# Mixer A on one Trainium2 core: scores from stacked rounded keys, queries split on POOL, and the division of the last pairs behind the values

## The chip, the core and the metric

The kernel runs on one core of one Trainium2 chip. Its engines are TensorE (PE; the profile lists its weight loads as PEld), VectorE (DVE), ScalarE (ACT), GpSimd (POOL) and SyncE (SP), whose queue issues all of the kernel's DMAs. Each engine takes its instructions in the order in which they were written for it and waits for the others by semaphores. The metric is the device time of one execution in microseconds; less is better.

## What is computed

One inference step of a one-layer streaming encoder on 1024 prompt tokens and 32 sample tokens, 1024 wide, all in fp32: a feed-forward network (FFN), two attention mixers side by side, a second FFN. Each of the three has its normalizations and its scale, shift and gate from a condition. Mixer A, cut to what matters:

```python
# mixer A: 8 heads of 64; a frame reads its own chunk of 64 and the 8 before it
def band_attn_a(qa, ka, va, bias, valid):
    s = einsum('bnqhd,bnkhd->bnhqk', qa, ka) * SCALE + bias
    s = where(valid, s, -1e30)
    p = softmax(s, axis=-1)
    return einsum('bnhqk,bnkhd->bnqhd', p, va)
# mixer B: 8 query heads on 2 key heads, own chunk and 2 before, with a sink in the softmax
o = concat(rmsnorm(oa, gains_a), rmsnorm(ob, gains_b)) @ w_out
```

The newest rows of the keys and values of both mixers are outputs too.

## The kernel before

Tokens lie in three blocks (384, 384 and 288 with the sample), features on partitions. A projection multiplies split operands: `split_w` and its like round a weight to fp32r on ACT (hi) and take the remainder on DVE (lo), and `mm3` sums hi x hi, hi x lo and lo x hi in three matmuls of fp32r. The FFNs, the input and the output projections are made that way (lines 325 to 327, and 669 to 671 for the values). Weights, keys, queries and values live in `wpool`, eight buffers of 8 KB per partition.

Between the FFNs stands the attention: a list of 72 tiles, each of 128 queries and one pair of heads. First come mixer B's four pairs, a sample tile (`TileS`) and eight of `TileB` each, then mixer A's pairs 0 and 1, a sample tile and eight of `TileA` each, then pairs 2 and 3 side by side. Tile `i` of mixer A reads up to 640 keys: its score length L is 128, 256, 384 and 512 for `i` from 0 to 3, and 640 from there on.

A tile of mixer A goes through these steps. `pre` makes a zero-padded copy `qz` of the queries for each head on POOL (lines 741, 742). `qk` multiplies it with the pair's keys in fp32 (line 752, in pieces of up to 512 columns), adds the bias and takes the maximum on DVE, takes the exponential on ACT with its sum (line 761), and divides P by that sum in one pass over it, on ACT or DVE (lines 764, 766). `tr` transposes P on PE (776) and copies PT out of PSUM, `av` multiplies PT with the values (713) into the one PSUM bank `po`, which ACT or DVE copies to O. In mixer B, `split_q` rounds the queries already, with SPLIT = "vav": a rounded copy on DVE, one on ACT and the remainder on DVE, into `qs`; its keys KSB are stacked, rounded keys on 64 partitions and their remainder on the other 64, so that two matmuls make the three products (813, 814).

```python
for e, o in ((SPLIT[0], T[hp, h, :]), (SPLIT[1], T[op, h, :])):
    ...
(ge if SPLIT[2] == "g" else ve).tensor_tensor(lo, q[hp], T[hp, h, :], op=OP.subtract)
```

Between the tiles stand other works, a little at each half tile: from tile 0 to 34 the projections of mixer B's other queries, of the values and of pair 0, from tile 37 to 54 those of pairs 1 to 3 (`pq`). Group norms begin at tile 55 (`sq`, `pss`, `pr`, `z`), and pieces of the output projection (`wo`) stand between the very last tiles. So pairs 2 and 3 have hardly any projections beside them. `k_rows` transposes the newest keys for the output (995). `qs`, PT, `sq`, `z`, the normalized `n` and the rows of keys share five buffers (`hpool`), `qz` has its own five (`spool`), scores have two pairs of PSUM banks.

The order of each engine isn't written out. The program names the steps in an order, and a planner that simulates the engines with its own costs then sets the sequence of each of them; only SP's queue is kept as written, up to the first FFN. So whatever changes a cost or a buffer can change the order on all engines.

## Time and profile before

| | us |
|---|---|
| median of 3 runs (lowest to highest) | 2216.33 (2215.64 to 2218.37) |
| the profiled execution | 2217.6 |
| its span, first to last instruction | 2215.8 |
| PE busy in it | 2161.6 (98%) |
| DVE, ACT, POOL busy | 1239.1, 697.8, 179.2 |

The profiled execution is 1.3 us above the median, and 1.8 us of it lie outside its span. To read the profile: a matmul is pipelined, so the duration of one is longer than its share of PE's time; what one of a row of equal matmuls costs is the distance of their starts. An fp32 matmul has two records in the trace, an fp32r matmul one. An idle time is put down to what ended last before it. The granted clock of PE is 1 at 2.4 GHz and 0.5 at 1.2 GHz.

### The profile page before, as it was taken

The page shows a single profiled execution, that of the slowest core. Times are in us where ns is not written, and L with a number is a line of the kernel's source. Part 1 is how long each engine was busy: PE and PEld are TensorE (multiplying, and loading weights), DVE is VectorE, ACT ScalarE, POOL GpSimd, SP SyncE. Part 2 cuts the span into 40 slices and gives each one's busy share as a digit, 9 for nine tenths or more (in the row PEclk, how much of TensorE's full clock was granted, in tenths as well). Part 3 has the DMA queues.
Part 4 walks back from the last instruction along what each step waited for, and adds up shares of the span by engine and source line. Part 5 has one row for each costly group of instructions (what it writes and reads, how often), then busy time and mean ns, then how long its engine had stood idle before and what let it go on. Part 6 is the DMA issues. An engine that isn't in the chain of part 4 may idle for free.

```text
span 2215.8 us, 33976 instructions
## 1 busy us (share of the span) xinstructions
PE 2161.6 (98%) x14012; PEld 2068.6 (93%) x14012; DVE 1239.1 (56%) x2425; ACT 697.8 (31%) x1450; POOL 179.2 (8%) x281
## 2 busy tenths in 40 slices
PE   6999999999999999899999899999999999999998
PEld 4999999999999999799787589999999999999998
DVE  5788667874333497677444865785333333333336
ACT  4411111111121253576444663542111111111133
POOL 1100000000000023001110313220000000000000
PEclk8999999999999999899999899999999999999999
DMA  9253334434122352111112121424211111111122
GB/s 323 93 153 118 111 96 124 143 101 129 39 66 69 101 184 93 38 39 30 50 30 62 46 77 67 134 86 120 66 58 39 57 39 39 58 38 58 39 69 79
DMA packets 200623, 186.03 MB, mean 84 GB/s; under 512 B 7597, under 2 KB 169813, under 8 KB 199317
## 3 DMA queue, kind: packets, MB, share of 16 engines
q1 hardware_dynamic: 200468, 183.87, 27.1%
q8 instruction: 110, 1.80, 0.3%
q14 instruction: 45, 0.36, 0.1%
HBM read 164.12 MB, written 22.86 MB: 84 GB/s over the span
## 4 chain that ended last, share of the span: by engine, by line
PE 90%; DVE 4%; DMA 3%; ACT 1%; issue 1%; POOL 0%; SPq 0%; ACTq 0%; DVEq 0%; POOLq 0%
PE dn L325 7%; PE dn L326 7%; PE dn L327 7%; PE gate L327 7%; PE gate L326 7%; PE up L327 7%; PE up L326 7%; PE gate L325 7%; PE up L325 7%; PE po L713 3%; PE S L752 2%; PE pq L325 2%; PE pq L327 2%; PE pq L326 2%; DMA raw<-in_w_gate_dram 1%; PE pp L776 1%
## 5 line engine op out<-in xcount | busy, mean ns | idle before, releaser
L326 PE MATMUL gate<-h_lo,w 128*128 128x384 f32 (+1 forms) x1056 | 340.2, 322 | 4.0 <-DVE h_lo L446 4.0
L325 PE MATMUL dn<-gg,w 128*128 128x384 f32 (+1 forms) x1056 | 341.4, 325 | 1.1 <-DVE facc L581 1.0
L581 DVE TENSOR_TENSOR facc<-dn,facc 128x768 f32<-128x768 f32 (+1 forms) x240 | 212.9, 889 | 230.2 <-PE dn L327 229.9
L326 PE MATMUL dn<-gg,w 128*128 128x384 f32 (+1 forms) x1056 | 340.6, 323 | 0.6 <-DVE gg L554 0.6
L325 PE MATMUL gate<-h_hi,w 128*128 128x384 f32 (+1 forms) x1056 | 341.0, 323 | 0.0
L327 PE MATMUL gate<-h_hi,w 128*128 128x384 f32 (+1 forms) x1056 | 340.4, 322 | 0.0
L325 PE MATMUL up<-h_hi,w 128*128 128x384 f32 (+1 forms) x1056 | 340.2, 322 | 0.0
L326 PE MATMUL up<-h_lo,w 128*128 128x384 f32 (+1 forms) x1056 | 340.0, 322 | 0.0
L327 PE MATMUL dn<-gg,w 128*128 128x384 f32 (+1 forms) x1056 | 340.0, 322 | 0.0
L327 PE MATMUL up<-h_hi,w 128*128 128x384 f32 (+1 forms) x1056 | 339.9, 322 | 0.0
L304 DVE TENSOR_TENSOR w<-raw,w 128x1024 fp32r<-128x1024 f32 x187 | 231.5, 1246 | 150.5 <-ACT w L303 150.3
L303 ACT ACTIVATE w<-raw 128x1024 fp32r<-128x1024 f32 x187 | 195.7, 1056 | 266.1 <-PE dn L327 103.5
L550 ACT ACTIVATE sl<-gate 128x384 f32<-128x384 f32 (+1 forms) x132 | 60.9, 462 | 563.9 <-PE gate L327 560.9
L551 DVE TENSOR_TENSOR sl<-sl,up 128x384 f32<-128x384 f32 (+1 forms) x132 | 68.5, 519 | 292.1 <-PE up L327 286.1
L326 PEld LDWEIGHTS gate<-h_lo,w 128*128 128x128 f32 x1056 | 198.6, 188 | 4.6 <-DVE h_lo L446 4.6
L325 PEld LDWEIGHTS dn<-gg,w 128*128 128x128 f32 x1056 | 199.2, 189 | 1.6 <-DVE facc L581 1.2
L326 PEld LDWEIGHTS dn<-gg,w 128*128 128x128 f32 x1056 | 199.2, 189 | 1.0 <-DVE gg L554 0.9
L327 PEld LDWEIGHTS dn<-gg,w 128*128 128x128 f32 x1056 | 199.1, 189 | 0.0
L325 PEld LDWEIGHTS gate<-h_hi,w 128*128 128x128 f32 x1056 | 198.7, 188 | 0.1
L327 PEld LDWEIGHTS gate<-h_hi,w 128*128 128x128 f32 x1056 | 198.7, 188 | 0.0
L327 PEld LDWEIGHTS up<-h_hi,w 128*128 128x128 f32 x1056 | 198.7, 188 | 0.0
L325 PEld LDWEIGHTS up<-h_hi,w 128*128 128x128 f32 x1056 | 198.5, 188 | 0.0
(224 smaller groups left out, 3367.4 us busy)
## 6 DMA issues: line engine op xcount, KB each, us to landing
raw<-in_w_mod_dram SPq DMA_DIRECT2D x56, 512.0 KB, 4.0
raw<-in_w_gate_dram SPq DMA_DIRECT2D x54, 512.0 KB, 4.0
raw<-in_w_up_dram SPq DMA_DIRECT2D x54, 512.0 KB, 4.7
raw<-in_w_down_dram SPq DMA_DIRECT2D x54, 512.0 KB, 4.5
raw<-in_w_in_dram SPq DMA_DIRECT2D x18, 512.0 KB, 4.3
wm<-in_w_mod_dram SPq DMA_DIRECT2D x8, 1024.0 KB, 7.4
raw<-in_w_out_dram SPq DMA_DIRECT2D x13, 512.0 KB, 4.5
xr<-xs SPq DMA_DIRECT2D x16, 384.0 KB, 3.5
```

The costliest lines, as they stand in the source:

```text
L303: ae.activation(w[:, 0], r, AF.Copy)
L304: ve.tensor_sub(w[:, 1], r, w[:, 0])
L325: te.matmul(ps, w[:, 0, k], hi, start=start, stop=False)
L326: te.matmul(ps, w[:, 0, k], lo, start=False, stop=False)
L327: te.matmul(ps, w[:, 1, k], hi, start=False, stop=stop)
L550: ae.activation(sl[:, :w], ps[0][:, :w], AF.Silu)
L551: ve.tensor_tensor(sl[:, :w], sl[:, :w], ps[1][:, :w], op=OP.mult)
L581: ve.tensor_tensor(o, ps[:, :, :w], o, op=OP.add)
L713: te.matmul(po[64 * h:64 * h + 64, :n], vsl(j, h, kn), PT(h, j, kn), start=j == 0, stop=j == nt - 1)
L752: te.matmul(S[:, c:ce], self.T[:, h, :], KQ[:, 0, 128 * k0 + c:128 * k0 + ce], start=True, stop=True)
L776: te.transpose(pp[:, j - j0, :], P[:, 128 * j:128 * j + 128], ident)
```

## The change

The scores of mixer A are made as those of mixer B already were. For each head of a pair the key projection leaves a stacked tile `KS`: ACT rounds the head's keys onto its own 64 partitions, DVE writes the remainder onto the other 64. `pre` fills `qs` with `split_q`: rounded queries on both halves, their remainder on one, zeros on the other. `qk` then takes two fp32r matmuls for each piece of keys; a length of 640 is cut in two pieces of 320, each in a bank of its own, and the shorter lengths are one piece. `k_rows` gets the keys back with a matmul against `twice`, two identities on top of each other, which adds the two halves.

SPLIT becomes "ggg": both rounded copies and the remainder of a query come from POOL, in mixer A and in mixer B. From RNORM = 2 on (pairs 2 and 3) P isn't divided. The reciprocals of a tile's two sums go through two small fp32 matmuls, which lay them along the queries in the same bank `po`; ACT copies them to O, and DVE multiplies the values' product by them.

`wpool` has sixteen buffers of 4 KB in place of eight of 8 KB, and everything in it is cut to that size: a weight's hi and lo are two tiles, a pair's keys two and its queries one, w_mod's first chunks come in four DMAs of half the size.

```diff
+RNORM = 2
...
-SPLIT = "vav"
+SPLIT = "ggg"
...
-    wpool = ctx.enter_context(tc.tile_pool(name="wpool", bufs=8))
+    wpool = ctx.enter_context(tc.tile_pool(name="wpool", bufs=16))
...
+    twice = consts.tile([128, 64], F32R, name="twice")
+    for h in range(2):
+        ae.activation(twice[64 * h:64 * h + 64], ident[64 * h:64 * h + 64, 64 * h:64 * h + 64], AF.Copy)
...
-        w = wpool.tile([128, 2, 8, 128], F32R, name="w", tag="w")
-        ae.activation(w[:, 0], r, AF.Copy)
-        ve.tensor_sub(w[:, 1], r, w[:, 0])
+        w = [wpool.tile([128, 8, 128], F32R, name="w", tag="w") for _ in range(2)]
+        ae.activation(w[0], r, AF.Copy)
+        ve.tensor_sub(w[1], r, w[0])
...
+                if put and not st:
+                    put(ps[:, a:b], slice(t0 + a, t0 + b))
+                    continue
...
-    def av(PT, L, vsl, O_dst, n=128):
+    def av(PT, L, vsl, O_dst, n=128, rden=None):
         po = pc("po")
+        if rden is not None:
+            for h in range(2):
+                te.matmul(po[64 * h:64 * h + 64, 128:256], rden[:, h:h + 1].to_broadcast([128, 64]), ident,
+                          start=True, stop=True)
         nt = (L + 127) // 128
         for j in range(nt):
             kn = min(128, L - 128 * j)
             for h in range(2):
                 te.matmul(po[64 * h:64 * h + 64, :n], vsl(j, h, kn), PT(h, j, kn), start=j == 0, stop=j == nt - 1)
-        evac(O_dst, po[:, :n])
+        if rden is None:
+            evac(O_dst, po[:, :n])
+        else:
+            ae.activation(O_dst, po[:, 128:256], AF.Copy)
+            ve.tensor_tensor(O_dst, po[:, :n], O_dst, op=OP.mult)
...
-            T = self.T = s_tile([128, 2, 128], "qz")
-            cols = slice(128 * self.i, 128 * self.i + 128)
+            q = kqa[self.p]["q"][:, 128 * self.i:128 * self.i + 128]
+            T = self.T = h_tile([128, 4, 128], "qs", F32R)
             for h in range(2):
-                hp, op_ = slice(64 * h, 64 * h + 64), slice(64 - 64 * h, 128 - 64 * h)
-                ge.memset(T[op_, h, :], 0.0)
-                ge.tensor_copy(T[hp, h, :], kqa[self.p][0][hp, 1, cols])
+                ge.memset(T[64 - 64 * h:128 - 64 * h, 2 + h, :].bitcast(F32), 0.0)
+                split_q(T, h, q, T[64 * h:64 * h + 64, 2 + h, :])

         def qk(self, h):
             p, i, k0, L = self.p, self.i, self.k0, self.L
-            KQ = kqa[p][0]
+            K = kqa[p]["k"][h]
             bias = prep[("A", p)]["bias"]
             bw = min(L, 256)
-            S = p2("S", (128, 1024))
-            for c in range(0, L, 512):
-                ce = min(L, c + 512)
-                te.matmul(S[:, c:ce], self.T[:, h, :],
-                          KQ[:, 0, 128 * k0 + c:128 * k0 + ce], start=True, stop=True)
-            ve.tensor_tensor(S[:, L - bw:L], S[:, L - bw:L], bias[:, h, 256 - bw:256], op=OP.add)
+            m = (L + 511) // 512
+            S = p2("S")[:, :m, :L // m]
+            for c in range(m):
+                keys = K[:, 128 * k0 + c * L // m:128 * k0 + (c + 1) * L // m]
+                te.matmul(S[:, c], self.T[:, h, :], keys, start=True, stop=False)
+                te.matmul(S[:, c], self.T[:, 2 + h, :], keys, start=False, stop=True)
+            near = S[:, m - 1, L // m - bw:L // m]
+            ve.tensor_tensor(near, near, bias[:, h, 256 - bw:256], op=OP.add)
             if i >= 4:
-                ve.memset(S[64:128, 0:64], NEG)
+                ve.memset(S[64:128, 0, 0:64], NEG)
             nm = small.tile([128, 1], F32, name="nm")
-            ve.tensor_reduce(nm, S[:, :L], axis=AX.X, op=OP.max, negate=True)
-            den = small.tile([128, 1], F32, name="den")
+            ve.tensor_reduce(nm, S, axis=AX.XY, op=OP.max, negate=True)
+            if p >= RNORM:
+                if h == 0:
+                    self.rden = small.tile([128, 2], F32, name="rden")
+                den = self.rden[:, h:h + 1]
+            else:
+                den = small.tile([128, 1], F32, name="den")
             P = g_tile([128, 640], "P")
-            ae.activation(P[:, :L], S[:, :L], AF.Exp, bias=nm, accum_out=den)
+            ae.activation(P[:, :L].rearrange("p (c n) -> p c n", c=m), S, AF.Exp, bias=nm, accum_out=den)
             ve.reciprocal(den, den)
-            if (2 * i + h) % SC[1] < SC[0]:
+            if p >= RNORM:
+                pass
+            elif (2 * i + h) % SC[1] < SC[0]:
                 ae.activation(P[:, :L], P[:, :L], AF.Copy, scale=den)
             else:
                 ve.tensor_scalar(P[:, :L], P[:, :L], den, None, op0=OP.mult)
...
-               lambda j, h, kn: vt[:, k0 + j, vo + 64 * h:vo + 64 * h + 64],
-               O[tb][:, p, 128 * c:128 * c + 128])
+               lambda j, h, kn: vt[(k0 + j) // 4][:, (k0 + j) % 4, vo + 64 * h:vo + 64 * h + 64],
+               O[tb][:, p, 128 * c:128 * c + 128], rden=self.rden)
...
-        if p % 2 == 0:
-            qb["t"] = wpool.tile([128, 2, 1024], F32, name="qbt", tag="w")
-        qt = qb["t"][:, p % 2, :]
+        qt = wpool.tile([128, 1024], F32, name="qbt", tag="w")
...
-        KQ = wpool.tile([128, 2, 1024], F32, name="KQ", tag="w")
+        KS = [wpool.tile([128, 1024], F32R, name="KS", tag="w") for _ in range(2)]
         KQs = small.tile([128, 2, DEC], F32, name="KQs", bufs=3)
-        kqa[p] = (KQ, KQs)
-        piece = qk_proj(w, KQ[:, 0, :], KQs[:, 0, :], 1.0)
+        kqa[p] = {"k": KS, "s": KQs}
+
+        def put(ps, cols):
+
+            for h in range(2):
+                hp, op = slice(64 * h, 64 * h + 64), slice(64 - 64 * h, 128 - 64 * h)
+                ae.activation(KS[h][hp, cols], ps[hp], AF.Copy)
+                ve.tensor_tensor(KS[h][op, cols], ps[hp], KS[h][hp, cols], op=OP.subtract)
+
+        piece = qk_proj(w, None, KQs[:, 0, :], 1.0, put)
         for tb in range(3):
             yield from piece(tb)

     def flow_qa(p, w):
-        KQ, KQs = kqa[p]
-        piece = qk_proj(w, KQ[:, 1, :], KQs[:, 1, :], 0.125)
+        Q = kqa[p]["q"] = wpool.tile([128, 1024], F32, name="Q", tag="w")
+        piece = qk_proj(w, Q, kqa[p]["s"][:, 1, :], 0.125)
         for tb in range(3):
             yield from piece(tb)

     def k_rows(p):
-        KQ, KQs = kqa[p]
+        KS, KQs = kqa[p]["k"], kqa[p]["s"]
         kr = h_tile([128, 4, 128], "kr")
         pk = (p1 if PB[0] else pc)("pkr", (128, 4, 128))
         for j in range(4):
-            te.transpose(pk[:, j, :], KQ[:, 0, 512 + 128 * j:640 + 128 * j], ident)
+            for h in range(2):
+                te.matmul(pk[:, j, 64 * h:64 * h + 64], KS[h][:, 512 + 128 * j:640 + 128 * j], twice,
+                          start=True, stop=True)
...
-        if p % 2 == 0:
-            prep["aux"] = wpool.tile([128, 2, 2, 4, 128], F32, name="aux", tag="w")
-        aux = prep["aux"][:, p % 2]
+        aux = wpool.tile([128, 2, 4, 128], F32, name="aux", tag="w")
```

PE's order in pairs 2 and 3, some tiles of 640 columns, before (S are the scores, pp the transposes, po the values, pr a group norm):

```order
L752 MATMUL S<-KQ,qz 128x512
L752 MATMUL S<-KQ,qz 128x128
L776 MATMUL pp<-ident,P 128x128 x5
L713 MATMUL po<-PT,vt 64x128 x8
L752 MATMUL S<-KQ,qz 128x512
L752 MATMUL S<-KQ,qz 128x128
L776 MATMUL pp<-ident,P 128x128
L713 MATMUL po<-PT,vt 64x128
```

The same place after, where rden are the reciprocals:

```order
L766 MATMUL S<-KS,qs 128x320
L767 MATMUL S<-KS,qs 128x320
L766 MATMUL S<-KS,qs 128x320
L767 MATMUL S<-KS,qs 128x320
L798 MATMUL pp<-ident,P 128x128 x5
L718 MATMUL po<-ident,rden 64x128 x2
L724 MATMUL po<-PT,vt 64x128
L766 MATMUL S<-KS,qs 128x320
L767 MATMUL S<-KS,qs 128x320
L766 MATMUL S<-KS,qs 128x320
L767 MATMUL S<-KS,qs 128x320
```

A head's two fp32 matmuls became four fp32r ones, and the reciprocals' two stand ahead of a tile's values.

POOL's order where the first FFN's end meets mixer B, before (h_lo is the remainder of the normalized input of the last block, which the projections need):

```order
L799 MEMSET qs 64x256
L449 TENSOR_TENSOR h_lo<-n,h_hi 128x256
L449 TENSOR_TENSOR h_lo<-n,h_hi 128x32
L799 MEMSET qs 64x256 x2
L449 TENSOR_TENSOR h_lo<-n,h_hi 128x256
L449 TENSOR_TENSOR h_lo<-n,h_hi 128x32
L799 MEMSET qs 64x256 x29
```

After:

```order
L821 MEMSET qs 64x256
L738 CAST qs<-qbt 64x128 x4
L739 TENSOR_TENSOR qs<-qbt,qs 64x128 x2
L453 TENSOR_TENSOR h_lo<-n,h_hi 128x256
L453 TENSOR_TENSOR h_lo<-n,h_hi 128x32
L821 MEMSET qs 64x256
L738 CAST qs<-qbt 64x128 x4
L821 MEMSET qs 64x256
L738 CAST qs<-qbt 64x128 x4
L739 TENSOR_TENSOR qs<-qbt,qs 64x128
L453 TENSOR_TENSOR h_lo<-n,h_hi 128x256
L453 TENSOR_TENSOR h_lo<-n,h_hi 128x32
```

Each B tile's memset got four casts and two differences behind it, and the second h_lo now follows two such groups.

## Rows read from the trace of the kernel before

**Rows 1.** Page, parts 1 and 4: busy us, share, instructions; the chain by engine.
```profile
PE 2161.6 (98%) x14012; PEld 2068.6 (93%) x14012; DVE 1239.1 (56%) x2425; ACT 697.8 (31%) x1450; POOL 179.2 (8%) x281
...
PE 90%; DVE 4%; DMA 3%; ACT 1%; issue 1%; POOL 0%; SPq 0%; ACTq 0%; DVEq 0%; POOLq 0%
```
**Rows 2.** Stretches (us): length; busy of PE, PEld, DVE, ACT, POOL; clock; DMA share; GB/s.
```profile
940.00:1064.00 124.00, 122.20 (x987) 110.53 (x987) 92.97 (x334) 87.45 (x306) 10.22 (x36) 1.00 0.12 33
1064.00:1215.00 151.00, 147.30 (x988) 120.03 (x987) 68.65 (x168) 68.16 (x174) 18.71 (x66) 0.99 0.16 44
1215.00:1250.00 35.00, 30.03 (x179) 18.80 (x180) 27.70 (x77) 23.85 (x65) 15.15 (x37) 0.76 0.35 100
1250.00:1290.00 40.00, 38.61 (x257) 26.40 (x257) 33.30 (x98) 27.39 (x61) 11.01 (x25) 1.00 0.00 1
```
**Rows 3.** PE in order of time, pair 1: start us, us, instruction, count.
```profile
1179.74 0.34 PE L325 MATMUL pq<-h_hi,w 128*128 128x384 f32 x1
...
1181.30 1.24 PE L752 MATMUL S<-KQ,qz 128*128 128x512 f32 x4
1182.38 0.60 PE L776 MATMUL pp<-ident,P 128*128 128x128 f32 x4
1182.74 0.42 PE L325 MATMUL pq<-h_hi,w 128*128 128x384 f32 x1
```
**Rows 4.** The same view, projections of 288 columns, nine matmuls apart.
```profile
1201.54 0.30 PE L325 MATMUL pq<-h_hi,w 128*128 128x288 f32 x1
...
1202.74 1.24 PE L752 MATMUL S<-KQ,qz 128*128 128x512 f32 x4
```
**Rows 5.** PE in order of time, mixer B: first tiles of two head pairs.
```profile
955.19 0.28 PE L814 MATMUL Sb<-KSB,qs 128*128 128x128 f32 x1
...
955.42 0.27 PE L814 MATMUL Sb<-KSB,qs 128*128 128x128 f32 x1
...
993.28 0.27 PE L814 MATMUL Sb<-KSB,qs 128*128 128x128 f32 x1
```
**Rows 6.** PE in order of time, pair 1: values of a tile.
```profile
1187.13 1.09 PE L713 MATMUL po<-PT,vt 128*64 128x128 f32 x14
1188.15 0.44 PE L325 MATMUL pq<-h_hi,w 128*128 128x384 f32 x1
```
**Rows 7.** POOL's groups, whole span: count | busy us, mean ns | idle before.
```profile
L368 POOL TENSOR_TENSOR sq<-sq 128x384 f32<-128x384 f32 x32 | 35.3, 1116 | 1422.0 <-ACT sq L364 1400.0 <-PE S L752 13.3 <-DVE w L304 5.0
...
L742 POOL COPY qz<-KQ 64x128 f32<-64x128 f32 x64 | 22.9, 358 | 2.8
...
L368 POOL TENSOR_TENSOR sq<-sq 128x288 f32<-128x288 f32 x16 | 14.7, 926 | 71.8 <-ACT sq L364 60.1 <-DVE gg L554 11.7
...
L741 POOL MEMSET qz<- 64x128 f32 x64 | 12.9, 202 | 164.0 <-PE S L752 82.6 <-PE pkr L1001 50.1 <-ACT o L705 14.6
L799 POOL MEMSET qs<- 64x256 f32 x32 | 10.2, 318 | 141.9 <-PE po L713 68.8 <-PE Sb L814 44.6 <-ACT vt L673 4.2
```
**Rows 8.** Line 742 alone: count, min/median/max ns; busy us in one stretch.
```profile
L742 POOL COPY qz<-KQ x64: 282/287/1671, 1048.5 to 1282.8; 64x128 f32<-64x128 f32 x64
...
1215.00:1250.00 35.00, 4.81 (x16) 0.76 0.35 100
```
**Rows 9.** PE's waits, 1215 to 1250 us: total, times, longest us.
```profile
PE S L752 <- ACT P L761: 1.6, 3, 0.9
PE pp L776 <- ACT P L764: 1.5, 1, 1.5
PE pp L776 <- DVE P L766: 1.2, 1, 1.2
```
**Rows 10.** Groups by shape, 1211 to 1330 us: DVE's division of 640 columns.
```profile
L766 DVE TENSOR_SCALAR P<-P,den 128x640 f32<-128x640 f32 x10 | 6.8, 675 | 0.2
```
**Rows 11.** POOL in order of time, 1223.5 to 1228 us.
```profile
1223.88 1.96 POOL L368 TENSOR_TENSOR sq<-sq 128x384 f32<-128x384 f32 x2 [5.61 <-PE S L752]
```
**Rows 12.** DVE in order of time, same place.
```profile
1224.16 0.80 DVE L766 TENSOR_SCALAR P<-P,den 128x128 f32<-128x128 f32 x1
```

More of the change, by code (lines that the diff above doesn't have):

```diff
@@ L139, in encoder_step @@
         XIN[0] = load_x(0)
-    jp = consts.tile([128, 128], I32, name="jp")
+    jp = s_tile([128, 128], "jp", I32)
     ge.iota(jp, pattern=[[1, 128]], base=0, channel_multiplier=-1)
@@ L176, in mod_chunk @@
         raws = []
-        for g in range(2):
-            r = wpool.tile([128, 4, 512], F32, name="wm", tag="w")
-            dma.dma_start(r, w_mod[0, 512 * g:512 * (g + 1), 512 * n:512 * (n + 1)]
+        for g in range(4):
+            r = wpool.tile([128, 2, 512], F32, name="wm", tag="w")
+            dma.dma_start(r, w_mod[0, 256 * g:256 * (g + 1), 512 * n:512 * (n + 1)]
                           .rearrange("(k p) n -> p k n", p=128))
@@ L185, in mod_chunk @@
                 k = 2 * g + kk
-                te.matmul(pm[32 * g:32 * g + 32, :], csil[:, k, :], raws[k // 4][:, k % 4, :],
+                te.matmul(pm[32 * g:32 * g + 32, :], csil[:, k, :], raws[k // 2][:, k % 2, :],
                           start=kk == 0, stop=kk == 1)
@@ L317, in split_vcols @@
             dma.dma_start(r, wm[0, 512 * h:512 * h + 512, c0:c0 + 256].rearrange("(k p) n -> p k n", p=128))
-            w = wpool.tile([128, 2, 4, 256], F32R, name="w", tag="w")
-            ae.activation(w[:, 0], r, AF.Copy)
-            ve.tensor_sub(w[:, 1], r, w[:, 0])
+            w = [wpool.tile([128, 4, 256], F32R, name="w", tag="w") for _ in range(2)]
+            ae.activation(w[0], r, AF.Copy)
+            ve.tensor_sub(w[1], r, w[0])
             out.append(w)
@@ L324, in mm3 @@
     def mm3(ps, w, k, hi, lo, start, stop):
-        te.matmul(ps, w[:, 0, k], hi, start=start, stop=False)
-        te.matmul(ps, w[:, 0, k], lo, start=False, stop=False)
-        te.matmul(ps, w[:, 1, k], hi, start=False, stop=stop)
+        te.matmul(ps, w[0][:, k], hi, start=start, stop=False)
+        te.matmul(ps, w[0][:, k], lo, start=False, stop=False)
+        te.matmul(ps, w[1][:, k], hi, start=False, stop=stop)
     def rsqrt(v, n, m):
@@ L668, in piece @@
                 a, b = hi[:, k, c0:c0 + n], lo[:, k, c0:c0 + n]
-                te.matmul(ps[:n, :256], a, wt[:, 0, kk], start=k == 0, stop=False)
-                te.matmul(ps[:n, :256], a, wt[:, 1, kk], start=False, stop=False)
-                te.matmul(ps[:n, :256], b, wt[:, 0, kk], start=False, stop=k == KT - 1)
-            o = vs if t == SEQ else vt[:, t // 128, :]
+                te.matmul(ps[:n, :256], a, wt[0][:, kk], start=k == 0, stop=False)
+                te.matmul(ps[:n, :256], a, wt[1][:, kk], start=False, stop=False)
+                te.matmul(ps[:n, :256], b, wt[0][:, kk], start=False, stop=k == KT - 1)
+            o = vs if t == SEQ else vt[t // 512][:, t // 128 % 4, :]
             ae.activation(o, ps[:n, :256], AF.Copy)
@@ L676, in v_proj, with qk_proj @@
         return piece
-    def qk_proj(w, dst, dst_s, scale):
+    def qk_proj(w, dst, dst_s, scale, put=None):
         def piece(tb):
@@ L812, in qk @@
                 cols = slice(128 * k0, 128 * k0 + L)
-                te.matmul(S[:, h, :L], T[:, h, :], KSB[:, c, cols], start=True, stop=False)
-                te.matmul(S[:, h, :L], T[:, 2 + h, :], KSB[:, c, cols], start=False, stop=True)
+                te.matmul(S[:, h, :L], T[:, h, :], KSB[c][:, cols], start=True, stop=False)
+                te.matmul(S[:, h, :L], T[:, 2 + h, :], KSB[c][:, cols], start=False, stop=True)
             ve.tensor_tensor(S[:, :, :L], S[:, :, :L], bias[:, :, 256 - L:256], op=OP.add)
@@ L868, in qk @@
             if kind == "A":
[L869 removed]
+                qs, kc, ks, sk = kqa[p]["s"][:, 1, :], pr["kc"], kqa[p]["s"][:, 0, :], None
             else:
@@ L949, in start_va @@
     def start_va(g, ws):
-        vt = wpool.tile([128, 8, 256], F32, name="vt", tag="w")
+        vt = [wpool.tile([128, 4, 256], F32, name="vt", tag="w") for _ in range(2)]
         vs = small.tile([32, 256], F32, name="vs", bufs=3)
@@ L1032, in encoder_step @@
     wkv, wq0, wv0 = split_vcols(w_in, 2048), load_qb(0), load_va(0)
-    kvb = wpool.tile([128, 8, 256], F32, name="vt", tag="w")
+    kvb = [wpool.tile([128, 4, 256], F32, name="vt", tag="w") for _ in range(2)]
     kvbs = small.tile([32, 256], F32, name="vs", bufs=3)
@@ L1056, in keys_new @@
         for j in range(n):
-            te.transpose(pk[:, j, :], kvb[:, t0 + j, 0:128], ident)
+            te.transpose(pk[:, j, :], kvb[t0 // 4][:, j, 0:128], ident)
         for c in range(2):
@@ L1060, in keys_new @@
             pkc = pk[64 * c:64 * c + 64, 0:n].rearrange("p a b -> p (a b)")
-            ae.activation(KSB[0:64, c, cols], pkc, AF.Copy)
-            ve.tensor_tensor(KSB[64:128, c, cols], pkc, KSB[0:64, c, cols], op=OP.subtract)
+            ae.activation(KSB[c][0:64, cols], pkc, AF.Copy)
+            ve.tensor_tensor(KSB[c][64:128, cols], pkc, KSB[c][0:64, cols], op=OP.subtract)
     def keys_sample():
@@ L1083, in encoder_step @@
         if tb == 2:
-            KSB = wpool.tile([128, 2, 1024], F32R, name="KSB", tag="w")
+            KSB = [wpool.tile([128, 1024], F32R, name="KSB", tag="w") for _ in range(2)]
             if PRIME:
```

11 lines of the change are left out of this document (5 added, 6 removed).

## The prediction

> **What bounds the kernel now.** The page comes first: TensorE (PE) is busy for 98% of the span and the chain that ended last runs through PE for 90% of it [rows 1]. So time can be saved only where PE has less to do or waits less, and work on another engine costs nothing until PE waits for it. The table of stretches says where that holds [rows 2]. Mixer B (940 to 1064 us) and pairs 0 and 1 of mixer A (1064 to 1215) are PE's: 122.2 of 124 and 147.3 of 151 us, at a granted clock of 1.00 and 0.99. The beginning of the last two pairs (1215 to 1250) is another matter: PE 30.0 of 35 at a granted clock of 0.76, POOL 15.2, DVE 27.7. There the chain score, maximum, exponential, division, transpose is what takes the time. PE's waits of that stretch say so: 1.6 us for the exponential, 1.5 and 1.2 us for the division of P on ACT and on DVE [rows 9]. From 1250 on PE is at 38.6 of 40 again. The two FFNs are not touched.
>
> **Scores in rounded pairs.** There are 64 heads of tiles (4 pairs, 2 heads, 8 tiles). In each set of 8 tiles the lengths are 128, 256, 384, 512 and four times 640, so eight sets in all. Before, a 640-column head stands on PE from 1181.30 to the transposes at 1182.38, 1.08 us, or 1.69 ns a column [rows 3]; each fp32 matmul is two records there. I take the other lengths at that price: 0.864, 0.648, 0.432 and 0.216 us. After, a head is two matmuls over the same columns with rounded operands. The projections already are such matmuls: nine of 384 columns fill 1179.74 to 1181.30, 0.173 each [rows 3], nine of 288 fill 1201.54 to 1202.74, 0.133 each [rows 4]; that is 0.417 ns a column and 13 ns. 320 columns then take 0.147, 512 take 0.227, 256 take 0.120. At 128 the rule ends: mixer B's scores of 128 columns follow at 0.115 [rows 5], as slow per column as fp32. A head saves 1.08 - 4 x 0.147 = 0.49 (640), 0.41, 0.30, 0.19 and, at 128, -0.01 us. A set saves 4 x 0.49 + 0.41 + 0.30 + 0.19 - 0.01 = 2.86 us, eight sets **22.9 us**, 11.45 in pairs 0 and 1 and 11.45 in pairs 2 and 3. Half of it meets a stretch that PE bounds.
>
> **Rows of the keys.** Four transposes (0.36 us, as from 1182.38 to 1182.74 [rows 3]) become eight matmuls of 64 rounded columns. No row has that form; the nearest is 0.115 for 128 columns, which gives 0.92 and is the upper end, and the lower end is no more than before. I take +0.4, nearer to the one row there is, for each of 4 pairs: **+1.6** (0 to +2.2), all before 1215.
>
> **Division behind the values, pairs 2 and 3.** Two matmuls of 64x128 in fp32 are added to each of 16 tiles, four records. The values have that shape: 14 records from 1187.13 to 1188.15, 0.073 each [rows 6]. 16 x 4 x 0.073 = **+4.7 us** (up to 0.108 a record, half of the 0.216 above, which makes 6.9). 32 passes over P go, 20 on DVE (0.675 us for the ten long ones [rows 10]) and 12 on ACT; a product of 128x128 on DVE comes for each tile. The copy to O was there; but PSUM's one bank for po is now held through ACT's copy and DVE's product.
>
> **POOL.** All of the split queries go there. A copy of 64x128 took 0.358, a memset 0.202 or 0.318; a difference of 64x128 isn't in the trace, and the line through 288 and 384 columns (0.926, 1.116) gives 0.61 at 128 [rows 7]. A B tile then costs 0.318 + 4 x 0.358 + 2 x 0.61 = 2.97 us, an A tile 0.40 + 1.43 + 1.22 = 3.05, where a qz cost 1.12. That a copy which rounds and changes partitions costs what L742 does is the assumption; the bounds are 0.282 and 1.67, its shortest and its longest, and its median of 0.287 [rows 8] is why I stay at the mean. In B a tile has (993.28 - 955.42)/8 = 4.7 us [rows 5], so POOL keeps up. In the first 35 us of the last pairs it does not have much room: of its 15.2 us 8 tiles were qz (16 copies [rows 8]), 9.0 us; 8 x 3.05 = 24.4 makes 30.6 of 35. At the change of stage ahead of B, POOL's second h_lo now stands behind two groups of copies where two memsets stood: 2 x (0.318 + 1.43) + 0.61 - 2 x 0.318 is 3.5 us later at most, and what PE needs of it are v-projections of the last block, of which other k and other token tiles are ready. I take **+1.5** (0 to +5) for that and for what B's tiles lose. B itself gives nothing: ACT and DVE get rid of their split, but PE was at 122.2 of 124.
>
> **Rounded keys** cost ACT one more pass and DVE two for each of 12 blocks of K, of 384 columns or fewer and so below the 0.675 us of 640 [rows 10], where DVE is at 68.6 of 151 and ACT at 68.2 [rows 2]: nothing, hidden behind the projections that follow on PE; without that cover up to 2 us a block, 24 in all. The 4 KB tiles hold as much as before; a pair's keys and query take 12 KB instead of 8, so wo has one weight fewer ahead. The DMA engines are at 16% there [rows 2]: nothing. At the start, w_mod's pieces are halved, the bytes remain: 0 (-1.5 to +1.5).
>
> **The sum.** Pairs 0 and 1: -11.45 + 1.6 = **-9.9**. Last pairs, first 35 us (lengths to 384): PE loses 4 x (0.30 + 0.19 - 0.01) = 1.9 and gains 6 x 0.29 = 1.7; the division leaves the chain, which is worth 2.7 us of the waits [rows 9] and some clock, and POOL at 87% and five h buffers, which now hold qs beside PT, sq and z, take it back: **0** (-6 to +8). Last pairs, the rest: -(11.45 - 1.9) + 10 x 0.29 = **-6.6** (-8 to -4). With +1.5: **-15.0 us**. The profiled execution took 2217.6 (span 2215.8), so 2202.6; the median of the runs is 2216.33, 1.3 below it, so **2201** for the median.
>
> **What speaks against it on POOL.** DVE's division of 128 columns took 0.80 us at 1224.16 [rows 12], more than the mean of 640 columns (0.675 [rows 10]); POOL ran two differences then, from 1223.88 to 1225.84 [rows 11]. The Trainium skill, SBUF — State Buffer, section SBUF: two separate sides, says why: VectorE and GpSimd share a pair of SBUF ports as a lock for a whole instruction, which a VectorE operation takes when it runs on two ports or reads two SBUF inputs, and the loser waits it out. The trace agrees with 0.80 against 0.675. By the row alone I price nothing in B; by the rule each of DVE's passes of that kind could lose up to one POOL operation, 0.61, which only matters where DVE is late for PE.
>
> **Rivals.** (1) The last pairs don't follow. POOL's 3 us a tile, the one bank of po or the h buffers set the pace of the first 35 us, and what PE saves later is waited away. For it: 30.6 of 35 for POOL, PE's clock of 0.76; against it: two division waits fall away. With +8 and -1 there instead of 0 and -6.6 the sum is -1.4, 2215; with +2.5 and -2 it is -7.9, 2208, the middle of this case. (2) The chain gets shorter by more than I count: the waits of 2.7 us and half of the lost clock (0.24 of 35 us, 8.4) come back, about -7: 2194. (3) Slower: POOL paces mixer B. Its place is the queue of copies ahead of each Sb; from 4.7 us a tile on, that is a copy of 0.79 instead of 0.358, PE waits for every tile. To eat the gain and 0.2% more it must lose (15 + 4.4)/32 = 0.6 a tile, a copy of 0.94. With the longest copy seen (1.67) for all of them a tile takes 8.2 us: 32 x 3.5 = +112, 2313; with 1.0 it is +27, 2228. For it is that a copy of L742 was once held to 1.67 [rows 8]; against it that the mean stayed at 0.358. The lock of which the Trainium skill tells (the same page and section) would be how a copy is held that long. (4) It doesn't do what it says: 320 columns cost on the chip what 128 do per column. Then a head's four matmuls take 4 x 0.288 = 1.15 against 1.08, a set 0.42 more instead of 2.86 less, and the sum is -15.0 + 22.9 + 3.4 = +11.3, 2228. The 288 and 384 columns speak against it.
>
> **How the numbers follow.** Forecast 0.50 (2196 to 2207), rival 1 0.27, rival 2 0.15, rival 3 0.06, rival 4 0.02. About 0.2%, 4.4 us, is what a measurement of this kernel can tell from no change, so faster means below 2211.9. Forecast, rival 2 and a little over half of rival 1 are faster: 0.50 + 0.15 + 0.16 = 0.81; the rest of rival 1 is the same, with 0.01 of the others: 0.12; slower is 0.07. The range from 2190 to 2214 takes in rival 2 but for its lower edge and rival 1 but for its slowest quarter; 0.19 stays outside.
>
> **What would show it.** Right: a 640-column head of 0.59 us on PE and pairs 0 and 1 about 10 us shorter; POOL's copies of 64x128 at 0.29 to 0.40; no PE wait for qs in B; the last pairs, from there to their last score, about 7 us shorter. Wrong: PE waiting for POOL qs (rival 3, or 1 if only in the last pairs), for po's release by DVE, or for PT's buffer; scores at more than 0.15 for 320 columns; a lower clock in the last pairs than 0.76, by which a PE with less work would give back what it saved.

## The result, and the profile after

The changed kernel takes 2223.47 us (median of 5 runs, 2221.18 to 2225.75) against 2215.64 for the kernel before (five runs beside it): a ratio of 1.0041, interval 1.0027 to 1.0054. It is 7.8 us slower. The forecast was 2201, the range ended at 2214, and slower had a chance of 0.07.

The page of after, its first part and the engines of the chain that ended last, answers [rows 1]:

```profile
span 2220.7 us, 34363 instructions
...
PE 2149.3 (97%) x14092; PEld 2074.6 (93%) x14092; DVE 1218.1 (55%) x2314; ACT 676.3 (30%) x1391; POOL 304.4 (14%) x601
...
PE 86%; DVE 6%; DMA 3%; ACT 2%; issue 1%; POOL 1%; SPq 0%; DVEq 0%; ACTq 0%; POOLq 0%
```

PE is busy 12 us less, as meant, and the span is 5 us longer: PE's share of the chain fell from 90 to 86%. The same stretches as in [rows 2], columns as there:

```profile
940.00:1064.00 124.00, 122.85 (x976) 109.96 (x975) 75.67 (x230) 71.70 (x248) 64.61 (x183) 1.00 0.11 33
1064.00:1215.00 151.00, 145.28 (x1056) 127.12 (x1056) 83.22 (x204) 78.49 (x208) 41.22 (x128) 0.98 0.16 44
1215.00:1250.00 35.00, 27.76 (x209) 19.74 (x207) 23.32 (x68) 20.09 (x56) 23.51 (x59) 0.80 0.35 99
1250.00:1290.00 40.00, 35.48 (x291) 29.43 (x290) 30.51 (x95) 24.84 (x61) 25.82 (x64) 0.96 0.01 1
```

From 1250 on PE, at 38.6 of 40 before, is at 35.5: part of the time that the scores gave up became waits.

A busy PE hides waits as well, since the profile's matmuls overlap. So I also gave every matmul the usual distance of starts of its shape where PE waited for nothing, and summed: this is an estimate of the work of a stage, and its length less the work is lost time. The level of the lost time depends on which distance is taken as the usual one: with the median by tile and shape, the kernel before loses 6.6 us in pairs 0 and 1 and 23.2 in the last pairs, not 17.3 and 36.9. The differences between the columns then agree with the table within 1 us, so only differences are used. The stages run between the first matmuls of each kind: mixer B's first score, mixer A's first score, the sample scores of pair 2, FFN2's first gate, the end of the span. Length (lost), in us:

| stage | before | after | E1: tiles alone | E2: tiles and keys |
|---|---|---|---|---|
| start, FFN1, change of stage | 917.0 (59.0) | 924.7 (66.7) | 921.6 (63.6) | 924.2 (66.2) |
| mixer B | 151.0 (23.8) | 152.2 (24.6) | 152.0 (24.8) | 151.7 (24.4) |
| pairs 0 and 1 | 144.1 (17.3) | 138.3 (21.3) | 141.9 (15.1) | 140.8 (22.8) |
| pairs 2 and 3, wo | 202.1 (36.9) | 200.6 (42.7) | 201.0 (35.8) | 210.7 (56.0) |
| FFN2 and end | 801.6 (20.7) | 804.8 (24.0) | 804.3 (23.4) | 803.8 (23.0) |

By this estimate PE's work fell by 16.6 us from before to after, as the prediction's terms have it. Lost time rose by 21.6: 7.7 ahead of mixer B and 3.3 in FFN2, for which the prediction has +1.5 and 0, 4.0 in pairs 0 and 1, 5.8 in the last pairs, 0.8 in B.

### The profile page after: what moved, and what is told of

Same layout as the page of the kernel before. It is cut to its first block, busy times and chain, and to the rows that moved or that the text cites. A ratio compares the mean times of both kernels' runs of the same rounds, so it can differ in the third digit from the quotient of the medians.

```text
span 2220.7 us, 34363 instructions
## 1 busy us (share of the span) xinstructions
PE 2149.3 (97%) x14092; PEld 2074.6 (93%) x14092; DVE 1218.1 (55%) x2314; ACT 676.3 (30%) x1391; POOL 304.4 (14%) x601
## 4 chain that ended last, share of the span: by engine, by line
PE 86%; DVE 6%; DMA 3%; ACT 2%; issue 1%; POOL 1%; SPq 0%; DVEq 0%; ACTq 0%; POOLq 0%
PE dn L329 7%; PE dn L330 7%; PE dn L331 7%; PE gate L330 7%; PE up L330 7%; PE gate L331 7%; PE up L329 7%; PE up L331 7%; PE gate L329 7%; PE po L724 2%; PE pq L329 2%; PE pq L330 2%; PE pq L331 2%; PE pv L675 1%; PE pp L798 1%
## 5 line engine op out<-in xcount | busy, mean ns | idle before, releaser
L372 POOL TENSOR_TENSOR sq<-sq 128x384 f32<-128x384 f32 (+1 forms) x48 | 51.9, 1091 | 1476.7 <-ACT sq L368 1468.3
L331 PEld LDWEIGHTS up<-h_hi,w 128*128 128x128 f32 x1056 | 198.9, 188 | 0.0
L330 PEld LDWEIGHTS up<-h_lo,w 128*128 128x128 f32 x1056 | 198.7, 188 | 0.0
```

Of the source, the lines that this page charges most:

```text
L330: te.matmul(ps, w[0][:, k], lo, start=False, stop=False)
L331: te.matmul(ps, w[1][:, k], hi, start=False, stop=stop)
L372: e.tensor_tensor(sq[:, 0, :w], sq[:, 0, :w], sq[:, 1, :w], op=OP.add)
```

## The experiments

Theory A: the 4 KB weight tiles give the planner another order, and the stages with unchanged code pay for it. Theory B: the loss is made in the mixers, by POOL's split and by the division. Each ratio is to runs of the kernel before on the same chip, and the interval is that of the ratio. The kernel before took 2215.52 to 2216.72 us beside the rows, which were not all measured on one chip, so a difference of two rows is not good to less than about 1 us.

| run | what | us | ratio to before (interval) |
|---|---|---|---|
| E1 | before + 4 KB tiles | 2223.94 | 1.0034 (1.0021 to 1.0046) |
| E2 | E1 + stacked keys in all pairs | 2231.03 | 1.0063 (1.0050 to 1.0076) |
| E3 | E2 + division behind the values | 2229.56 | 1.0057 (1.0044 to 1.0070) |
| E4 | E2 + split on POOL | 2223.61 | 1.0032 (1.0019 to 1.0044) |
| after | E2 + both | 2223.47 | 1.0041 (1.0027 to 1.0054) |
| E5 | after, pairs 2 and 3 without the split (remainder left out) | 2214.34 | 0.9995 (0.9986 to 1.0003) |
| E12 | before + split on POOL (mixer B) | 2224.75 | 1.0049 (1.0036 to 1.0063) |
| E13 | E1 + keys in pairs 0 and 1 only | 2217.16 | 1.0007 (0.9999 to 1.0016) |
| E14 | before + division | 2222.57 | 1.0034 (1.0022 to 1.0046) |

**E1, the tiles alone.**

```diff
-    wpool = ctx.enter_context(tc.tile_pool(name="wpool", bufs=8))
+    wpool = ctx.enter_context(tc.tile_pool(name="wpool", bufs=16))
-        w = wpool.tile([128, 2, 8, 128], F32R, name="w", tag="w")
+        w = [wpool.tile([128, 8, 128], F32R, name="w", tag="w") for _ in range(2)]
```

> The kernel before with nothing but its 8 KB weight tiles cut into 4 KB tiles (16 buffers; w_mod in quarters, rounded and remaining half of a weight apart, query and keys apart, vt, kvb, KSB and aux in halves). Theory A (the tiles reorder stages whose code is not touched): the trace of after lost 1.9 us up to 100 us, 1.3 in FFN1, 4.5 between FFN1 and the first Sb, 3.3 at the opening of FFN2, in all 11.0 us, and the program's PE order in both FFNs differs from before in the same way for this kernel as for after; so it should be 6 to 11 us slower than before, 2222 to 2227, with the 3.3 us wait for h_lo at FFN2's opening. Theory B (the loss is made by the mixer's own edits, POOL and the division): within 3 us of before.

It is 7.2 us slower than before. By the table it loses 4.6 us ahead of mixer B, 1.0 in B and 2.7 in FFN2, and gains 3.3 in mixer A. The opening of FFN2 shows how. PE in order of time, first of before, then of E1, then of after (start us, us, instruction, count, idle before it and its releaser):

```profile
1436.48 0.99 PE L405 MATMUL pr<-ident,ry 128*128 128x128 f32 x6
...
1442.92 0.45 PE L326 MATMUL gate<-h_lo,w 128*128 128x384 f32 x1 [2.13 <-DVE h_lo L446]
```

```profile
1440.77 0.83 PE L405 MATMUL pr<-ident,ry 128*128 128x128 f32 x6
1442.95 0.45 PE L325 MATMUL gate<-h_hi,w 128*128 128x384 f32 x1 [1.35 <-ACT h_hi L444]
...
1447.05 0.69 PE L326 MATMUL gate<-h_lo,w 128*128 128x384 f32 x1 [3.30 <-DVE h_lo L446]
```

```profile
1441.16 0.83 PE L409 MATMUL pr<-ident,ry 128*128 128x128 f32 x6
1443.35 0.44 PE L329 MATMUL gate<-h_hi,w 128*128 128x384 f32 x1 [1.35 <-ACT h_hi L448]
...
1447.45 0.69 PE L330 MATMUL gate<-h_lo,w 128*128 128x384 f32 x1 [3.30 <-DVE h_lo L450]
```

`pr` lays the second block's reciprocal norms along the tokens; the chain to h_hi and h_lo waits for it. In before it stands behind 8 of the 24 `dn` matmuls of the first block, in E1 and after behind all 24, and PE then waits 4.7 us for the second block instead of 2.1. The code of FFN2 is the same in all three. The start is alike. Its first 100 us, columns as in [rows 2], in before, in E1 and in after:

```profile
0.00:100.00 100.00, 81.25 (x459) 66.54 (x460) 62.29 (x140) 45.41 (x81) 17.53 (x22) 0.91 0.67 230
```

```profile
0.00:100.00 100.00, 77.85 (x445) 64.21 (x446) 64.69 (x142) 45.67 (x82) 20.20 (x24) 0.93 0.67 230
```

```profile
0.00:100.00 100.00, 78.39 (x447) 64.52 (x448) 65.03 (x143) 46.10 (x84) 20.20 (x24) 0.93 0.67 230
```

PE idles 22.1 us there in E1 and 21.6 in after, and 18.7 in before. At the change of stage, from 800 us to B's first score, single waits move and their sum grows less: 7.2 us before, 7.8 in E1, 8.6 in after. Theory A holds for the start and for FFN2. After loses 3.1 us more than E1 ahead of mixer B, which the tiles alone don't explain; E2, with all keys stacked, loses nearly as much (924.2 against 924.7), and why is open.

**E2, the keys with no POOL and no division** (`SPLIT = "vav"`, `RNORM = 4` in after).

> After without the division behind the values (no pair uses it) and without the split on POOL (ACT, ACT and DVE split as in mixer B of before): what is left is the 4 KB tiles and the stacked rounded keys. PE has 23 us less scores and 2.6 us more rows of keys. Theory A: about -20 + 9 and some waits in mixer A, 2207 to 2213. Theory B: 2196 to 2203, what the prediction had without its other terms.

Both theories were wrong: PE has 19 us less work than in E1, and the kernel is 7 us slower than E1. Pairs 2 and 3 alone grew by 9.7 us. The stretch from 1250 in E2, columns as in [rows 2], and PE's waits from 1208 to 1300 (us in total, times, longest):

```profile
1250.00:1290.00 40.00, 30.93 (x204) 22.98 (x200) 36.35 (x115) 26.98 (x64) 9.29 (x20) 0.83 0.00 1
```

```profile
PE S L766 <- ACT P L781: 7.3, 9, 1.5
PE po L724 <- DVE o L710: 2.2, 1, 2.2
PE pp L798 <- DVE P L788: 1.6, 1, 1.6
```

DVE is at 36.4 of 40: with the split of the queries it has become the busiest engine. E4, which takes the split from it, is 7.4 us faster. PE, at 30.9, runs at a granted clock of 0.83 where [rows 2] have 1.00.

**E3 and E4, one of the other edits each** (E3 is after with `SPLIT = "vav"`, E4 after with `RNORM = 4`).

> After with the queries split by ACT, ACT and DVE instead of POOL. If POOL is what cost mixer B 2.6 us, the transition 4.5 and the last pairs part of 5.3, this is 6 to 10 us faster than after, 2213 to 2217. If the tiles and the division are the cause, it is within 3 us of after, 2220 to 2226.

> After without the division behind the values. In after's trace PE waits 2.8 us for the product that frees po's bank and has 5 to 6 us of added matmuls; if the shorter chain of the last pairs gives nothing back, this is 5 to 8 us faster than after, 2215 to 2218. If the chain was worth its price, it is 0 to 5 us slower than after.

POOL's split gives 7.4 us on top of the keys (the intervals of E2 and E4 do not touch); the division gives nothing that can be told apart, with or without POOL. By the profiled runs 4.8 us of that gain lie in pairs 2 and 3 (205.9 against 210.7). E3 reads 6.1 us slower than after, against both of its expectations, though the two intervals overlap, and E4 equals after.

**E5, the last pairs without the split.** Both score matmuls read Q, once rounded, so the remainder of the query is left out:

```diff
+            if self.p >= 2:
+                self.T = q[:, None, :].to_broadcast([128, 4, 128])
+                return
```

> After, but pairs 2 and 3 do not split their queries: Q is written once rounded and both score matmuls take it (the remainder of the query is left out there, and with it POOL's memsets, copies and differences of 16 tiles, about 48 us of POOL, and the tile qs in the h buffers). PE has the same matmuls. Theory P (POOL's queue and the h buffers set the pace of the last pairs): their lost PE time falls from 34.8 us by 6 us or more, 2213 to 2217. Theory D (what paces them is the chain through DVE and ACT and the group norms in it): within 2 us of after, 2221.5 to 2225.

9.1 us faster than after, most of it in the last pairs (193.5 us against 200.6), with the same matmuls on PE. PE's waits in that stage are 16.7 us in after, 10.4 in E5 and 10.2 in before. Theory P holds there. In after PE's weight loads wait for the split, from 1208 to 1336 us (us in total, times, longest):

```profile
PEld S L766 <- POOL qs L739: 2.2, 3, 1.6
...
PEld S L766 <- POOL qs L738: 1.5, 2, 1.3
```

That is 3.7 us; in before they waited 2.3 us for POOL's `qz` there. POOL in order of time shows the queue:

```profile
1242.53 1.81 POOL L1183 TENSOR_TENSOR o_lo<-z,o_hi 128x768 fp32r<-128x768 f32 x1
1244.40 0.51 POOL L738 CAST qs<-Q 64x128 fp32r<-64x128 f32 x1
1244.97 0.20 POOL L754 MEMSET qs<- 64x128 f32 x1
1245.21 0.65 POOL L738 CAST qs<-Q 64x128 fp32r<-64x128 f32 x2
...
1248.96 0.45 POOL L739 TENSOR_TENSOR qs<-Q,qs 64x128 fp32r<-64x128 f32 x1
```

One group-norm difference of 1.8 us, and then the splits of more than a tile until 1249.4. E5 also frees the `h` buffers that held qs; the two were not separated. Nor has it the copies qz, which before has.

**E6, E8, E15: single steps of that chain.** E6 copies the reciprocals to O through a bank of ps1 ahead of the values, E8 puts `o_lo` on DVE (`GNP = ()`), E15 puts the cross copies of pairs 2 and 3 on ACT (`"gag"`).

> After with the reciprocal sums broadcast into a bank of the ps1 pool and copied to O ahead of the values, so that po's one bank is held by the values and DVE's product alone. PE waited 0.7 + 0.9 + 1.3 us for that product in the trace of after. If the bank is a bound of its own, 1.5 to 3 us faster than after, 2220.5 to 2222. If the wait only moves to the next step of the chain, within 1 us of after.

> After with the remainder o_lo of the group norms on DVE alone instead of POOL for every second piece. In after's chain POOL stood from 1242.5 to 1248.5 us, 1.82 us of it with o_lo and the rest with qs queued behind it. Theory P: 1 to 3 us faster than after, 2220.5 to 2222.5. Theory D (DVE is the engine that is short): 1 to 3 us slower than after, 2224.5 to 2226.5.

> After with the copies that cross the partitions in the queries' split of pairs 2 and 3 on ACT instead of POOL (two of eight POOL operations a tile, about 0.6 of 2.8 us). If POOL is the one that is short, 1 to 3 us faster than after, 2220 to 2222. If ACT, DVE and POOL are all in the chain and a step only changes place, within 1 us or up to 3 us slower, 2223 to 2226.

Measured 2222.30 (1.0033, 1.0021 to 1.0046), 2226.93 (1.0053, 1.0039 to 1.0068) and 2224.70 (1.0044, 1.0032 to 1.0056). E6 and E15 cannot be told from after; E8 looks slower by 3.5, though its interval overlaps after's. So taking a single step off POOL and giving it to DVE or ACT gained nothing that can be told; taking the whole split away gained 9.1 us, and moving it from ACT and DVE to POOL 7.4 (E4).

**E13, the keys where PE is the bound.** In after, with `SPLIT = "vav"` and `RNORM = 4`, pairs 2 and 3 have fp32 scores as before:

```diff
+        KS = wpool.tile([128, 1024], F32, name="KQ", tag="w") if p >= 2 else \
+            [wpool.tile([128, 1024], F32R, name="KS", tag="w") for _ in range(2)]
```

> After without POOL's split and without the division behind the values, with stacked rounded keys in pairs 0 and 1 only; pairs 2 and 3 have fp32 scores as before. It is the kernel of e1 with keys in two pairs. PE has 9.5 us less to do than in e1 in pairs 0 and 1. If PE bounds them, as the prediction had it, 5 to 9 us faster than e1, 2215 to 2219. If what e2 showed there is the rule (its pairs 0 and 1 took 133.6 us against 134.1 in e1), within 2 us of e1, 2222 to 2226.

2217.16 is 6.8 us below E1, within the 5 to 9 expected from PE's 9.5 us of work. By the ratios to before it is 6.0. So stacked keys pay in pairs 0 and 1. Giving them to pairs 2 and 3 too costs 13.9 (E2 less E13); by the profiled runs 9.3 of it lie in the last pairs (210.7 against 201.4) and 3.4 in pairs 0 and 1, where the later pairs' keys are projected.

**E12 and E14, the other two edits on the kernel before** (`SPLIT = "ggg"`; the division in pairs 2 and 3).

> The kernel before with nothing but the split of mixer B's queries on POOL (8 KB tiles, fp32 scores in mixer A, the FFNs' order as before). The prediction's terms: B itself 0, since POOL needs 3.0 of 4.7 us a tile, so within 3 us of before, 2214 to 2219. If POOL paces B, slower by 5 us or more; if ACT and DVE were what PE waited for, faster by 3 or more.

> The kernel before with nothing but the division behind the values in pairs 2 and 3 (and the iota of the identity in a passing buffer, for its room). PE gets 5 to 6 us of matmuls, the chain of the first 35 us loses a pass over P. On after's own base it gave 1.5 us with ACT and DVE splitting and 0.1 with POOL splitting. If the chain bounds the last pairs, 1 to 5 us faster than before, 2211 to 2215; if the matmuls and po's bank count, 1 to 4 us slower, 2217 to 2220.

Both are slower than the runs of before beside them: by 9.2 and 6.5 us. E12 lies outside the 3 us of the prediction's terms, and E14 beyond either of its expectations. E14's last pairs and wo take 207.1 us against 202.1. Its added matmuls take 0.27 us in most tiles and up to 0.48, 5.2 us in all, and PE's waits in that stage went from 10.2 to 12.0 us: the matmuls count, and the shorter chain gives nothing back. In E12 mixer B takes 157.8 us against 151.0, with one stall late in it,

```profile
1046.45 0.69 PE L842 MATMUL ppb<-ident,Pb 128*128 128x128 f32 x2 [1.67 <-ACT Pb L830]
```

and 3.4 us at a granted clock of 0.5 (1.2 GHz) from 1046.2 on. At B's opening that clock lasts 6.8 us instead of 3.4, and PE waits 2.6 us instead of 1.1 for a load of cached keys at its end; the rest of its loss lies in small pieces. On the 4 KB tiles the same split leaves B alone (150.7 in E4, 151.7 in E2). Why the one order is hurt and the other not stays open.

**E7, the opening of mixer A.** In after PE waits 3.27 us there for a bank of scores, where before waited 1.34. ACT and SP in order of time:

```profile
1079.41 1.06 ACT L307 ACTIVATE w<-raw 128x1024 fp32r<-128x1024 f32 x1 [1.14 <-DMA raw<-in_w_in_dram]
1080.38 0.69 ACT L910 ACTIVATE Ps<-Ss,nm 64x544 f32<-64x544 f32 x1
```

```profile
1074.94 0.36 SPq L1034 DMA_DIRECT2D out_dram<-kr  x1
1075.35 6.78 SPq L305 DMA_DIRECT2D raw<-in_w_in_dram  x4
```

The sample's exponential stands on ACT behind the rounding of a weight, which waits for its load, which stands on SP behind the rows of keys. E7 issues the two stores of rows from ACT (`ae.dma_start`).

> After with the two stores of each pair's rows of keys issued from ACT's queue instead of SP's, so that the loads of weights that stand behind them on SP do not wait for the rows. At the opening of mixer A PE waited 3.27 us for a bank of scores, whose exponential stood on ACT behind a weight's rounding that waited for its load. If the rows' place on SP made that load late, that wait falls to about 1.3 us and the kernel gains 2 to 5 us, 2218.5 to 2221.5. If the load is late for a buffer, no change (within 1 us).

The wait fell to 2.01 us and pairs 0 and 1 by 0.8; the total reads 2226.01 (1.0047, 1.0031 to 1.0062), which cannot be told from after. In the profiled run, the slowest of six, the last pairs, in an order that changed again, took 206.6 us instead of 200.6. The load's place is part of the wait; the gain was not kept.

**E9, E10, E11: the tiles undone in the FFNs.** The weight pool is closed and opened again at the mixers' borders, with 8 KB tiles outside. E10 adds E6's bank and a second score matmul of 64 rows without POOL's memsets; E11 has the keys in pairs 0 and 1 only.

> After with the weights of the start and of both FFNs in eight 8 KB tiles as before, and the sixteen 4 KB tiles only from the projections of the mixers to wo (the pool is closed and opened again at the two borders). The mixers do the same work. Theory A (the small tiles cost 7 us by the order they give the FFNs): the start gets back 2 us, FFN2's opening about 3 and the transition 0 to 3, 2214 to 2219. If the loss in the FFNs comes from the mixers' edits, 2222 to 2225.

> The kernel of e9 with two more edits in mixer A: the second score matmul takes only the 64 rows that are not zero, so that POOL's two memsets a tile fall away (0.4 of about 3 us), and the reciprocal sums go through a bank of ps1 as in e6. POOL's whole split of pairs 2 and 3 was worth 9 us in e5; 0.4 of 3 of that is 1.2, and e6 gave about 1. Theory P: 1 to 3 us faster than e9. If the split counts by its longest steps and not by POOL's sum, within 1 us of e9.

> The kernel of e9 with stacked rounded keys in pairs 0 and 1 only; pairs 2 and 3 have fp32 scores, qz on POOL and the division on P as before. Pairs 0 and 1 were 5 us shorter in after than in before, and the last pairs to FFN2's opening 2.1 us shorter. So if the traces add up, 1 to 4 us slower than e9 and 0 to 4 us faster than before. If the last pairs' keys cost more than they give, faster than e9.

2259.29, 2288.62 and 2236.13 us (ratios 1.0198, 1.0331 and 1.0093): the border has a price of its own, as two waits of E9 at FFN1's end show, and B is longer too (162.2 us against 152.2 in after).

```profile
843.56 0.85 PE L342 MATMUL dn<-gg,w 128*128 128x288 f32 x2 [3.82 <-ACT gg L570]
...
860.37 0.58 PE L689 MATMUL pv<-w,h_hi 128*128 128x256 f32 x1 [4.61 <-DVE w L337]
```

As a test of theory A these are inconclusive; E10 against E9 shows a cost of its own, told under the hardware.

**E16 and E17, towards a better kernel.** E16 is E13 with POOL's split in pairs 0 and 1; E17 is E16 with `OUTSTEP = 8`, which puts `pr` behind 6 `dn` matmuls.

> The kernel of e13 with the queries of pairs 0 and 1 split on POOL (mixer B's by ACT, ACT and DVE, pairs 2 and 3 with fp32 scores as before). Pairs 0 and 1 took 131.2 us in after and 131.9 in e4 with POOL's split, 133.6 and 133.8 in e2 and e3 without. So 0 to 3 us faster than e13: 2213 to 2217, and as good as before or better. If the gain of POOL's split lies in the last pairs alone, as e13's.

> The kernel of e16 with eight steps of side work behind each of the last pieces of wo instead of six. In PE's order six dn matmuls stand ahead of the three pr at FFN2's opening (24 in e16 and after, 8 in before). If the order there is what cost 3 us, the wait for h_lo falls from 3.3 to about 2 us and the one for h_hi goes: 2 to 4 us faster than e16, which would beat before. If the chain behind pr is late for another reason, within 1 us of e16.

2217.18 (1.0008, 0.9999 to 1.0017) and 2216.90 (1.0006, 0.9997 to 1.0015): neither can be told from E13 or from the kernel before. In E17 the two waits at FFN2's opening became one, and another came up in the stage ahead:

```profile
1347.17 0.76 PE L361 MATMUL pss<-ones,sq 128*128 128x1 f32 x6 [3.51 <-POOL sq L374]
...
1444.90 0.44 PE L330 MATMUL gate<-h_lo,w 128*128 128x384 f32 x1 [1.73 <-DVE h_lo L450]
```

FFN2 and the end took 796.8 us instead of 803.4 in E16, the last pairs and wo 209.5 instead of 203.7. The order at the opening is the cause of the waits there, and mending it alone moved the loss. None of these versions beat the kernel before.

## Why the prediction was wrong, point by point

The sum was -15 and the profiled run gives +4.8 by the table of stages. Of the miss of 20 us, 7.4 lie ahead of mixer A (+8.9 for +1.5), 4.1 in pairs 0 and 1 (-5.8 for -9.9), 5.1 in the last pairs (-1.5 for -6.6) and 3.2 in FFN2.

- **Scores in rounded pairs: right.** A 640-column head in after, PE in order of time, is four matmuls 0.147 apart, 0.58 us in all, as forecast:

```profile
1179.05 0.30 PE L766 MATMUL S<-KS,qs 128*128 128x320 f32 x1
1179.19 0.31 PE L767 MATMUL S<-KS,qs 128*128 128x320 f32 x1
1179.34 0.31 PE L766 MATMUL S<-KS,qs 128*128 128x320 f32 x1
1179.49 0.31 PE L767 MATMUL S<-KS,qs 128*128 128x320 f32 x1
1179.63 0.49 PE L798 MATMUL pp<-ident,P 128*128 128x128 f32 x3
```

- **Rows of keys and added matmuls of the division: right.** Eight matmuls of rows took 0.81 to 1.10 us where PE did not stall among them, for the 0.41 to 0.59 of four transposes, and the division's matmuls 5.1 us in all, for +4.7.
- **"The two FFNs are not touched", the start 0, the change of stage +1.5 at most 5: wrong, and the largest miss.** The 4 KB tiles were costed as memory alone (bytes, DMAs, one weight fewer ahead). They are also what the planner gives out and waits for, and with them it chose other orders in both FFNs, which the prediction does not price, though the text ahead of it says that a buffer can change the order on all engines. E1 puts the price of the tiles at 7.2 us. That this is close to the whole measured loss is chance: the gains and losses in mixer A happen to cancel. Why the planner chose so is not shown.
- **Pairs 0 and 1, -9.9: half right.** E13 gives 6.8 of it. In after the stage is 5.8 shorter. Of the 4.1 us that are missing, the wait at mixer A's opening is 1.9 (3.27 for 1.34). Around it the granted clock is 0.5 for 6.8 us instead of 3.4, by estimate 1.7 us more.
- **The rest of the last pairs, -6.6: wrong.** The forecast priced POOL's split in the first 35 us only, at POOL 30.6 of 35, and at nothing from 1250 on. POOL was at 23.5 of 35 and then at 25.8 of 40, where before had 11.0, and the saving was waited away. E5 measures what the split and its buffers take: without them the last pairs are 8.6 us shorter than before, with them 1.5. So the saving on PE could be had once the split was gone. Whether "PE is at 38.6 of 40 again" was a bound of the kernel before stays open: by distances of starts the matmuls of that stretch need 32.7 us, or 37.1 with the median by tile and shape, and E14, where 5.2 us of matmuls made the stage 5.0 longer, speaks for a bound. Rival 1 had this mechanism, and its middle, +0.5 for the last pairs, is near the -1.5 of the profiled run; it had deserved the larger chance.
- **Division behind the values, 0 in the first 35 us: too kind.** By itself it costs 6.5 us (E14); on the keys it gives nothing that can be told. PE waited 2.8 us for the product that frees po's bank, yet freeing the bank earlier (E6) gave no sure gain.
- **POOL's pace in B: the size was right, the verdict not.** Copies took 0.32 and differences 0.46 us, as forecast or less, and PE waits 0.9 us for qs in all of B. Yet the same edit on the kernel before costs 9.2 us (E12), 6.8 of it in B by the profiled runs. PE never waits for qs there; ACT waits 2.4 us for it to copy a PT, which takes its buffer from the same pool.
- **"What speaks against it on POOL": stronger than it was told.** What POOL ran at 1223.88 were two sums (line 368), not differences. The mean of 0.675 us for 640 columns holds one division of 1.82 us beside a POOL difference; the other nine average 0.55.

POOL's groups in mixer B of after (925 to 1060 us; count, busy us, mean ns, idle before), for the point on B:

```profile
L738 POOL CAST qs<-qbt 64x128 fp32r<-64x128 f32 x112 | 35.8, 320 | 6.3
L739 POOL TENSOR_TENSOR qs<-qbt,qs 64x128 fp32r<-64x128 f32 x55 | 25.3, 461 | 4.0
```

## What to carry to other kernels

Where a planner sets the order, a change of buffer sizes is a change of every stage that uses the buffers: compare the orders of the stages whose code is the same first, and price the waits that move. A saving on a PE that is 96% busy is kept only as far as the engines that must feed it keep up: price what the edit adds to them in every stretch, not only in the one where PE already waits. And a product made cheaper on PE by splitting its operand pays only where the split can hide; here the stacked keys gave 7 us in pairs 0 and 1 and cost 14 when pairs 2 and 3 had them too.
